# A two-layer hybrid transformer on one core: the last feed-forward sublayer by plain products instead of seven block products

## The chip, the core and the metric

The kernel runs on one core of a Trainium2 chip, as a single program. The core has a matrix engine (PE, with its weight loads shown apart as PEld), a vector engine (DVE), a scalar engine (ACT), a general engine (POOL), an engine that here issues the transfers (SP), and 16 DMA engines. The metric is the device time of one execution in microseconds. Three runs of the kernel before gave 3025.62, 3025.64 and 3031.76 us.

## The reference

Two streams, 512 tokens of `x` and 256 tokens of `ctx`, each 1024 wide, pass through two layers. A layer has three sublayers: a feed-forward one, a mixer (attention, state space and retention side by side), and a second feed-forward one. Only `x` is returned, so the last layer's second feed-forward sublayer works on 512 tokens alone.

```python
def swiglu(h, wg, wu, wd):
    return (jax.nn.silu(h @ wg) * (h @ wu)) @ wd

def sublayer_in(h, m, i):
    return h * (1.0 + m[..., i, 1, :]) + m[..., i, 0, :]

def residual(h, sub, m, i, g, b):
    return layer_norm(DEEPNORM_ALPHA * h + (1.0 + m[..., i, 2, :]) * sub, g, b)
...
        x = residual(x, 0.5 * swiglu(sublayer_in(x, m_l, 2), ffn_w_gate[l, 1], ffn_w_up[l, 1], ffn_w_down[l, 1]),
                     m_l, 2, norm_g[l, 2], norm_b[l, 2])
```

The gate and up weights are 1024 x 2816, the down weights 2816 x 1024, all in fp32.

## The kernel before

**Order of the work.** The six sublayers follow each other; sublayer (l, i) is layer l, place i, so the last one is (1, 2). The program is written as a sequence, but a planner orders each engine's instructions anew when it is built, by a simulated timeline (`schedule_with_timeline_sim=True`, L1669): what comes first in the text has priority, and what would have to wait in that simulation is passed by what is ready. On the chip each engine then runs its list strictly in that order. All transfers that matter here are on the queue of SP.

**Precision.** Every fp32 operand is split into two fp16 pieces, a first one (ACT, L320 for weights, L445 for activations) and the remainder (DVE, L321 and L446), and each product takes the three passes (first, first), (first, second), (second, first), `PASSES`. One block of pieces has 512 weight columns (or 2 x 256, or 4 x 128) on 128 partitions, with both pieces.

**Feed-forward sublayer (`ffn`, L357).** The 2816 hidden columns are 11 pairs of 128, and the pairs are in five groups, `GROUPS = [[0, 1], [2, 3], [4, 5], [6, 7], [8, 9, 10]]`. For each pair there are the gate and the up product, silu and their product; after each group the down products of its pairs are added to `acc`; after the last group comes the norm.

- *Seven products.* For pairs 1 to 10 the gate and up products go by Winograd's form of Strassen's scheme: the weights in four blocks (column tile, half of the features), the input in four blocks (half of the features, half of the tokens), and seven block products instead of eight. `load` (L408) makes the sums S1 to S4 of weight blocks on POOL (L414 to L417) and splits seven blocks into pieces. `gate_up` (L476) runs seven products of 12 matmuls each for gate and for up (L494) and combines them on DVE (L499, one copy on ACT, L510). The differences of the input's blocks are made once per sublayer by `input_differences` (L466, DVE and POOL L454 to L460) from an fp32 copy of the input that the norm before stored in DRAM (L301, `keep`) and that is loaded again (L472).
- *Down products of groups 0 to 3* go the same way: `prep_down` (L382) makes sums of weight blocks on POOL (L391 to L394) and seven blocks of pieces, `put_act` (L429) makes sums of activation blocks on POOL (L437 to L440) and seven blocks of pieces, and `down_blocks` (L705) runs seven products for each token tile of a half (L719) and combines them on DVE and POOL (L726, L731, L733, L734).
- *Plain form.* Pair 0 of every sublayer but the first goes by plain products (`gate_up_plain`, L541, matmuls L555): for each of two column tiles, gate and up with 8 feature tiles x 3 passes, into a PSUM buffer ("big", two of them) that holds both; `silu_up` (L424) then reads it. It leaves PE busy while the input differences are made. In the last sublayer it does the first three token tiles ahead of the fourth, which arrives late. The last group's down products are plain too (`down_last`, L768, matmuls L781).

**Buffers.** Raw weights come by transfers of 1 MB into two buffers ("raw"). Blocks of pieces have 16 buffers "pc", which all sublayers share, and 5 buffers "pcd" in the pool of the sublayer itself; `ring` (L372) deals them out in turn, in proportion. The sublayer's own pool can only be used once the sublayer before is done with its own. `load_plain` (L404) uses `prep` (L341), which takes "pc" buffers only.

**How far ahead.** `prepare` (L803) works off a list of jobs, one transfer of weights and its pieces each, in the order of use, and keeps `FIT` = 3 jobs ahead of the pair or group that uses them.

Of the kernel before, what the change touches and what calls it, by code (L numbers as in the profile page):

```python
# [43 lines left out]
def kernel(  # L44
# [25 lines left out]
    class Tags:  # L70
        """Allocators of one phase: a rotating set of buffers for each kind of use."""
# [36 lines left out]
    def condition(alloc):  # L108
        """Loads the vectors that the whole network needs as columns, and takes them to columns."""
# [39 lines left out]
        # ALPHA times the gains and biases of the norms, as rows in DRAM  # L149
# [5 lines left out]
    def ada_vec(l, v, alloc):  # L155
        """One conditioning vector of both streams."""
# [32 lines left out]
    def gate_bcast(l, i, n, alloc):  # L189
        """The scaled gate rows of sublayer (l, i) on all partitions, for each of n streams."""  # L190
        res = []
        for r in range(n):
            gt = alloc([P, D], f"gate{l}{i}{r}")
            nc.sync.dma_start(out=gt, in_=gate_rows[l, i][r].partition_broadcast(P))
            res.append(gt)
        return res

# [1 line left out]
    def affine_cols(l, i, prev):  # L199
        """Columns (scale, bias) that take the normalised rows to SA * (input of sublayer (l, i))."""  # L200
# [11 lines left out]
    def to_pieces(dst, src32):  # L212
        """src32 [P, KC, P] fp32 -> dst [P, 2, KC, P] fp16 pieces."""
        V.tensor_copy(dst[:, 0], src32)
        V.tensor_tensor(out=dst[:, 1], in0=src32, in1=dst[:, 0], op=ALU.subtract)

    def turn(yh, t, cols, nm, alloc):
        """Rows of tile t -> transposed fp32 input of a sublayer, in two halves of its features."""
# [22 lines left out]
    class Stream:  # L241
        """The residual stream between sublayers: ALPHA times its rows in DRAM (the first one's without ALPHA), and
        the sublayer's transposed input where that is wanted again."""
# [6 lines left out]
    class Norm:  # L250
        """The normalisation that ends sublayer (l, i), and what follows from it, tile by tile in two stages."""

        def __init__(self, l, i, nxt, last, arow, ayh, au32):
# [5 lines left out]
            if not last:  # L259
# [3 lines left out]
                self.keep = nxt[1] != 1  # L263

        def one(self, t, rt):
            """rt: the residual sum of tile t."""
# [45 lines left out]
    def block(shape, nm, dt=F16):  # L312
        """Room for the fp16 pieces of 512 weight columns (in several row tiles) or so."""
        return main.tile([P, 2] + shape, dt, tag="pc", name=f"pc{nm}", bufs=NBLOCK)
# [8 lines left out]
    class Pieces:  # L323
        """Pieces of a weight block, two row tiles in each buffer."""
# [7 lines left out]
    def load_raw(src, a, b, nm):  # L332
        """src may be a list of blocks that lie side by side."""
# [16 lines left out]
    # Gate and up products go by Winograd's form of Strassen's 2 x 2 x 2 scheme: with W^T in blocks A11, A12, A21, A22  # L350
    # (column tile, half of the features) and the input in B11, B12, B21, B22 (half of the features, half of the
    # tokens), seven block products of fp16 pieces give the four blocks of W^T u.
    # The down products of all but the last group of pairs go the same way: activations in blocks (half of the tokens,
    # column tile), weights in blocks (column tile, half of the output features).
    GROUPS = [[0, 1], [2, 3], [4, 5], [6, 7], [8, 9, 10]]

    def ffn(l, i, uT, stream, ntiles, nxt, last, todo):  # L357
# [5 lines left out]
        with tc.tile_pool(name=f"ffn{l}{i}", bufs=1) as fp:  # L363
# [8 lines left out]
            def ring(shape, nm):  # L372
                """A block of pieces from the two sets of buffers in turn, in proportion to their numbers."""
# [6 lines left out]
            plain = GROUPS[-1]  # L380
# [23 lines left out]
            def load_plain(pr_):  # L404
                wt[pr_] = [prep(columns(src, pr_), KC, 256, f"gu{l}{w}_{pr_}{q}")
                           for q, src in enumerate((ffn_w_gate, ffn_w_up))]

            def load(pr_, q):  # L408
                nm = f"gu{l}{i}_{pr_}{q}"
                raw = load_raw(columns((ffn_w_gate, ffn_w_up)[q], pr_), KC, 256, nm)  # L410
# [18 lines left out]
            def put_act(pr_, sg, spare):  # L429
                """Pieces of the activations sg of a pair, in blocks as its down products want them."""  # L430
# [17 lines left out]
            # differences of the input's blocks, as pieces  # L448
            tt = {}

            def differences(b11, b12, b21, b22, k, cols, shape, nm):
                """Blocks k, columns cols of the differences, from the fp32 input."""
# [23 lines left out]
            def gate_up(pr_):  # L476
# [5 lines left out]
                for q, dst in enumerate((sg, up)):  # L482
# [22 lines left out]
                    # the first pair leaves time for the differences, the last one starts with the first tokens  # L505
# [35 lines left out]
            def gate_up_plain(pr_):  # L541
# [17 lines left out]
                # the last token tile of a short stream comes late: it waits for the others' products  # L559
                if not has_ctx:  # L560
# [3 lines left out]
                for cc in range(2):  # L564
                    for pp, lo, hi in parts[cc]:
                        if not has_ctx:
# [6 lines left out]
            def first_pair():  # L573
                """The conditioning of the first sublayer, its input and its first pair of column blocks, which
                proceed together through the blocks of two feature tiles as these arrive."""
# [129 lines left out]
            def down_blocks(gi, prs):  # L705
                """Adds the down products of a group of pairs to acc."""
# [39 lines left out]

            def gate_rows_of(h):
# [7 lines left out]
            def residual(h):  # L755
                """Half h of acc: ALPHA times the stream plus the gated products so far."""
# [40 lines left out]
            # the weights go through the buffers in the order of their use  # L797
# [13 lines left out]
            else:  # L811
                load_plain(0)
                input_differences()
            prepare(FIT)
            for gi, prs in enumerate(GROUPS):
                for q in prs:
                    if todo and (q > 1 or len(todo) >= NPAIR - 1 - q):
                        ada_vec(*todo.pop(0), al("ada"))
                    if q > 0:
                        gate_up(q)  # L820
                    else:
                        if start:
                            finish()
                        else:
                            gate_up_plain(0)
# [5 lines left out]
                if gi < len(GROUPS) - 1:  # L831
                    down_blocks(gi, prs)
# [6 lines left out]
    class Fill:  # L839
        """Projection work that is laid between the steps of the chains, as generators that yield their cost."""  # L840
# [28 lines left out]
    class Skew:  # L869
        """Generators that advance together, each one step behind the one that came after it."""  # L870
# [20 lines left out]
    def mixer(l, uT, stream, nxt, last):  # L891
# [5 lines left out]
        with tc.tile_pool(name=f"mix{l}", bufs=1) as mp:  # L897
# [10 lines left out]
            # weights of the projections, in the order of their use  # L908
# [18 lines left out]
            def mm_T(pp, pc, cc, lo, hi):  # L927
                """Transposed projection of one 128-column chunk."""
# [8 lines left out]
            def mm_tok(pp, pc, t, n_=256):  # L937
                """Projection of 256 columns for one token tile."""
# [18 lines left out]
            # per-layer scalars on all partitions  # L957
# [39 lines left out]
            def rv_tile(t):  # L997
                """Values of the retention branch and raw steps of the state-space branch, one token tile."""
# [120 lines left out]
            def put_state(Hs, t, pst):  # L1119
                """The state of chunk t goes to the slot of the chunk that it enters."""  # L1120
# [94 lines left out]
            class Rope:  # L1215
                """A transposed projection whose first S columns are rotated."""
# [169 lines left out]
            def attend(h, t):  # L1386
# [21 lines left out]
                # both maps share the first one's row sum, which the output takes up  # L1408
# [265 lines left out]
```

## Time and profile before

| what | value |
|---|---|
| median of the runs | 3025.64 us |
| the profiled execution: span from its first to its last instruction | 3023.2 us |
| mean granted clock of PE | 0.966 |
| last feed-forward sublayer: first matmul of pair 0 | 2567.6 us |
| end of its pair 0, about | 2592.8 us |
| its last matmul ends | 3014.2 us |
| its matmuls, pairs 1 to 10 and down products | 2160 |

The page of a profile gives the busy time of each engine; a stretch of the span can be asked for alone. In a group of instructions the columns are line, engine, operation, output and inputs, shapes and count, then busy us and mean ns of one, then the idle time of the engine just before them and what ended it. In the order of time a row has start, length, engine, line, operation and count, and in brackets the idle time before it with the instruction that ended it. A matmul's own duration includes its way through the array, so rates are read from runs of many.

### The profile page before, as it was taken

To read this page: it belongs to the slowest core of one execution; us is meant where nothing else is said; L and a number is where in the kernel's file an instruction comes from. 1 tells how busy PE (TensorE), PEld (TensorE's weight loads), DVE (VectorE), ACT (ScalarE), POOL (GpSimd) and SP (SyncE) were. 2 spreads that over 40 slices of the span, in tenths; PEclk is the share of its full clock that TensorE was granted. 3 is DMA by queue.
4 is the path that set the end of the run, shared out by engine and by line. 5 is a ranking of instruction groups with operands and counts; after the bars stand their busy time and mean duration, and the time that the engine had idled before them with its cause. 6 is when DMAs were issued, how large, how long until landed. Compare 5 with 4: busy or idle time off the path is not lost. (4 is left out here: it accounts for less than half of the span.)

```text
span 3023.2 us, 45096 instructions
## 1 busy us (share of the span) xinstructions
PE 2666.6 (88%) x17087; PEld 1615.5 (53%) x17087; DVE 2538.8 (84%) x3677; ACT 1224.7 (41%) x2602; POOL 1544.6 (51%) x1296
## 2 busy tenths in 40 slices
PE   6799999989899979999999889888999998777778
PEld 4444444557677834444444444444556677555455
DVE  4988888886867788898789988898887777899998
ACT  3443343434447343343233443343335374444332
POOL 1646557132525464566725646567232444656672
PEclk9899999999999999999999999999999999899999
DMA  7253354333233253453372322122333342322222
GB/s 230 70 176 124 112 189 147 104 116 92 72 96 99 100 180 117 134 195 120 111 244 104 133 70 68 45 84 94 105 113 112 91 112 92 133 83 84 70 79 89
DMA packets 221519, 346.97 MB, mean 115 GB/s; under 512 B 16136, under 2 KB 162294, under 8 KB 221302
## 3 DMA queue, kind: packets, MB, share of 16 engines
q1 hardware_dynamic: 221302, 344.09, 35.3%
q8 instruction: 134, 2.20, 0.3%
q14 instruction: 83, 0.68, 0.1%
HBM read 303.52 MB, written 25.31 MB: 109 GB/s over the span
## 5 line engine op out<-in xcount | busy, mean ns | idle before, releaser
L494 PEld LDWEIGHTS <-pcgu 128*128 128x128 f16 x5088 | 500.4, 100 | 440.4 <-issue 181.2
L494 PE MATMUL m<-T,pcgu 128*128 128x384 f16 (+1 forms) x2400 | 410.7, 318 | 43.5 <-DVE U L499 31.1
L719 PE MATMUL pd<-pcd,act 128*128 128x512 f16 x1452 | 367.0, 392 | 76.9 <-DVE act L446 23.1
L719 PEld LDWEIGHTS <-act 128*128 128x128 f16 x1848 | 183.3, 100 | 343.2 <-issue 112.1
L494 PE MATMUL x<-uT,pcgu 128*128 128x384 f16 (+1 forms) x1512 | 254.8, 318 | 39.3 <-DVE sg L499 16.7
L321 DVE SCALAR_TENSOR_TENSOR pcgu<-rawgu,pcgu 128x512 f16<-128x512 f32 x208 | 237.6, 1156 | 16.6 <-ACT pcgu L320 16.4
L734 POOL TENSOR_TENSOR acc<-acc,D 128x512 f32<-128x512 f32 x132 | 188.9, 1443 | 71.0 <-DVE acc L733 70.6
L494 PEld LDWEIGHTS <-pegu 128*128 128x128 f16 x1632 | 160.4, 100 | 118.2 <-issue 36.0
L417 POOL TENSOR_TENSOR S4gu<-rawgu,S2gu 128x512 f32<-128x512 f32 x80 | 113.4, 1417 | 181.5 <-DVE pcgu L321 178.3
L414 POOL TENSOR_TENSOR S1gu<-rawgu 128x512 f32<-128x512 f32 x80 | 115.9, 1449 | 109.0 <-DMA rawgu<-in_ffn_w_gate_dram 55.5
L415 POOL TENSOR_TENSOR S2gu<-S1gu,rawgu 128x512 f32<-128x512 f32 x80 | 119.8, 1497 | 89.2 <-DVE pcgu L321 72.8
L416 POOL TENSOR_TENSOR S3gu<-rawgu 128x512 f32<-128x512 f32 x80 | 123.2, 1540 | 77.9 <-DVE pegu L321 54.5
L320 ACT ACTIVATE pcgu<-rawgu 128x512 f16<-128x512 f32 x208 | 125.6, 623 | 65.3 <-PE m L494 18.6
L942 PEld LDWEIGHTS <-uT 128*128 128x128 f16 x1344 | 133.7, 100 | 32.8 <-issue 12.6
L781 PE MATMUL pd<-pcd,act 128*128 128x512 f16 x594 | 144.7, 379 | 4.2 <-DVE dt L787 3.8
L94 POOL TENSOR_SCALAR rs<-mv 128x1 f32<-128x1 f32 x32 | 16.3, 508 | 240.5 <-DVE mv L273 240.5
L228 ACT ACTIVATE u<-pt,abc 128x128 f32<-128x128 f32 x224 | 81.5, 467 | 141.3 <-PE pt L225 95.5
L321 DVE SCALAR_TENSOR_TENSOR pcd<-rawd,pcd 128x512 f16<-128x512 f32 x132 | 135.4, 1039 | 0.8 <-ACT pcd L320 0.5
L446 DVE TENSOR_TENSOR act<-sg,act 128x384 f16<-128x384 f32 (+1 forms) x141 | 131.4, 963 | 2.2 <-ACT act L445 2.2
L781 PEld LDWEIGHTS <-act 128*128 128x128 f16 x792 | 77.4, 98 | 99.4 <-issue 12.6
L494 PE MATMUL x<-T,pcgu 128*128 128x384 f16 (+1 forms) x672 | 119.6, 320 | 11.8 <-DVE sg L499 6.5
L726 DVE TENSOR_TENSOR D<-D,pd 128x512 f32<-128x512 f32 x132 | 89.9, 681 | 46.6 <-PE pd L719 45.1
(375 smaller groups left out, 6403.5 us busy)
## 6 DMA issues: line engine op xcount, KB each, us to landing
adaw<-in_ada_w_dram SPq DMA_DIRECT2D x128, 512.0 KB
rawd<-in_ffn_w_down_dram SPq DMA_DIRECT2D x44, 1024.0 KB
rawgu<-in_ffn_w_gate_dram SPq DMA_DIRECT2D x43, 1024.0 KB
rawgu<-in_ffn_w_up_dram SPq DMA_DIRECT2D x43, 1024.0 KB
row<-yh SPq DMA_DIRECT2D x56, 256.0 KB
rawwo<-in_w_out_dram SPq DMA_DIRECT2D x8, 1024.0 KB
inp<-u SPq DMA_DIRECT2D x16, 512.0 KB
u<-inp SPq DMA_DIRECT2D x16, 512.0 KB
```

The lines of the kernel that those rows point to most:

```text
L320: A.activation(pc[:, 0], src, AF.Copy, scale=SW)
L321: V.scalar_tensor_tensor(out=pc[:, 1], in0=src, scalar=SW, in1=pc[:, 0], op0=ALU.mult, op1=ALU.subtract)
L414: G.tensor_tensor(out=s1, in0=a21, in1=a22, op=ALU.add)
L415: G.tensor_tensor(out=s2, in0=s1, in1=a11, op=ALU.subtract)
L416: G.tensor_tensor(out=s3, in0=a11, in1=a21, op=ALU.subtract)
L417: G.tensor_tensor(out=s4, in0=a12, in1=s2, op=ALU.subtract)
L446: V.tensor_tensor(out=pc[:, 1], in0=src, in1=pc[:, 0], op=ALU.subtract)
L494: PE.matmul(pp, lhsT=blocks[m][:, a, k, :], rhs=rhs, start=(n == 0), stop=(n == 11))
L719: PE.matmul(pd, lhsT=acts[q][m][:, a, ts], rhs=wd[q][m][:, b], start=(n == 0), stop=(n == len(prs) * 3 - 1))
L734: G.tensor_tensor(out=c_, in0=c_, in1=part, op=ALU.add)
L781: PE.matmul(pd, lhsT=acts[q][2 * cc + hf][:, a, o:o + P], rhs=wd[q][2 * cc + h][:, b], start=(n == 0), stop=(n == len(prs) * 6 - 1))
L942: PE.matmul(pp, lhsT=uT[:, a, k, t * P:(t + 1) * P], rhs=pc.at(b, k, 0, n_), start=(n == 0), stop=(n == KC * 3 - 1))
```

## The change

In the last feed-forward sublayer, (1, 2), all pairs and groups use the plain form. `gu_plain` and `plain` name the pairs whose weights and activations are split without sums: all of them there; in the other sublayers pair 0 (gate and up) and the last group (down), as before. `load` and `load_plain` now share one path, in which the blocks of plain weights come from `ring`, so also from "pcd" buffers; that holds for pair 0 in the sublayers (0, 2) and (1, 0) too. The mixer before the last sublayer no longer stores the fp32 input for the differences, and these are not made there. Only pair 0 still treats the late token tile apart. A new function, `down_plain`, adds the plain down products of groups 0 to 3: a matmul group of 12 per token tile and half of the output, copied to `acc` by ACT in group 0 and added by DVE afterwards.

```diff
-                self.keep = nxt[1] != 1
+                self.keep = nxt[1] != 1 and nxt != (DEPTH - 1, 2)
...
-            plain = GROUPS[-1]
+            whole_plain = not has_ctx
+            gu_plain = set(range(NPAIR)) if whole_plain else {0}
+            plain = set(range(NPAIR)) if whole_plain else set(GROUPS[-1])
...
             def load_plain(pr_):
-                wt[pr_] = [prep(columns(src, pr_), KC, 256, f"gu{l}{w}_{pr_}{q}")
-                           for q, src in enumerate((ffn_w_gate, ffn_w_up))]
+                for q in range(2):
+                    load(pr_, q)
 
             def load(pr_, q):
                 nm = f"gu{l}{i}_{pr_}{q}"
-                raw = load_raw(columns((ffn_w_gate, ffn_w_up)[q], pr_), KC, 256, nm)
+                src = columns((ffn_w_gate, ffn_w_up)[q], pr_)
+                if pr_ in gu_plain:
+                    raw = load_raw(src, KC, 256, nm)
+                    blocks = []
+                    for j in range(0, KC, 2):
+                        blocks.append(ring([2, 256], f"{nm}{j}"))
+                        split_weight(blocks[-1], raw[:, j:j + 2, :])
+                    wt.setdefault(pr_, []).append(Pieces(blocks))
+                    return
+                raw = load_raw(src, KC, 256, nm)
...
-                if not has_ctx:
+                late = not has_ctx and pr_ == 0
+                if late:
...
+            def down_plain(gi, prs):
+                for t in range(ntiles):
+                    hf, o = t // (ntiles // 2), (t % (ntiles // 2)) * P
+                    for h in range(2):
+                        pd = sm([P, 512], f"pd{l}{i}_{gi}{t}{h}")
+                        n = 0
+                        for q in prs:
+                            for cc in range(2):
+                                for a, b in PASSES:
+                                    PE.matmul(pd, lhsT=acts[q][2 * cc + hf][:, a, o:o + P],
+                                              rhs=wd[q][2 * cc + h][:, b],
+                                              start=(n == 0), stop=(n == len(prs) * 6 - 1))
+                                    n += 1
+                        c_ = acc[t][:, h * 512:(h + 1) * 512]
+                        if gi == 0:
+                            A.copy(c_, pd)
+                        else:
+                            V.tensor_tensor(out=c_, in0=c_, in1=pd, op=ALU.add)
...
                 load_plain(0)
-                input_differences()
+                if not whole_plain:
+                    input_differences()
...
-                    if q > 0:
-                        gate_up(q)
+                    if start and q == 0:
+                        finish()
                     else:
-                        if start:
-                            finish()
-                        else:
-                            gate_up_plain(0)
+                        (gate_up_plain if q in gu_plain else gate_up)(q)
+                    if q == 0:
                         new_acc()
...
-                    down_blocks(gi, prs)
+                    (down_plain if whole_plain else down_blocks)(gi, prs)
```

The other lines of the diff take out comments and docstrings.

More of the change, by code (lines that the diff above doesn't have):

```diff
@@ L565, in gate_up_plain @@
                     for pp, lo, hi in parts[cc]:
-                        if not has_ctx:
+                        if late:
                             mm(pp, cc, S - P, S, S - P)
```

## The prediction

> **What bounds the kernel now.** First the page's totals, then the busy time of each engine in stretches, for all engines are loaded in a mean over stages that differ.
>
> ```profile
> span 3023.2 us, 45096 instructions
> ...
> PE 2666.6 (88%) x17087; PEld 1615.5 (53%) x17087; DVE 2538.8 (84%) x3677; ACT 1224.7 (41%) x2602; POOL 1544.6 (51%) x1296
> ```
>
> Stretches (columns: stretch, length, PE, weight loads, DVE, ACT, POOL busy with counts, granted clock, DMA share, GB/s):
>
> ```profile
> 2593.00:3014.20 421.20, 325.95 (x2160) 218.77 (x2159) 393.60 (x539) 162.77 (x322) 248.50 (x179) 0.92 0.27 87
> ...
> 2593.00:2620.00 27.00, 9.81 (x62) 6.46 (x62) 26.04 (x25) 14.69 (x30) 20.61 (x14) 0.81 0.45 158
> ...
> 2991.00:3014.00 23.00, 23.00 (x108) 10.29 (x106) 21.75 (x34) 0.41 (x1) 5.62 (x6) 1.00 0.18 69
> 1656.00:1686.00 30.00, 28.53 (x185) 18.20 (x184) 25.58 (x28) 11.84 (x27) 20.45 (x15) 1.00 0.63 228
> ...
> 1095.00:1615.00 520.00, 470.77 (x2892) 234.03 (x2891) 446.83 (x601) 190.60 (x344) 279.19 (x204) 0.98 0.45 151
> ```
>
> The first row is the sublayer that is changed, from the end of its pair 0 to its last matmul. DVE is busy 393.6 of 421.2 us (93%), PE 77% at a clock of 0.92. So VectorE sets the pace. What PE waits for there says the same:
>
> ```profile
> PE m L494 <- DVE U L499: 19.0, 11, 3.4
> PE pd L719 <- DVE act L446: 18.2, 15, 2.6
> ...
> PE pd L719 <- DVE pcd L321: 6.0, 1, 6.0
> ```
>
> The long waits are for combinations of products and for activation pieces. For weight pieces PE waited 6.0 us, once. Why DVE is so slow shows in its costliest instruction, the second piece of a weight block (L321), in this sublayer and in the mixer (min/median/max ns):
>
> ```profile
> L321 DVE SCALAR_TENSOR_TENSOR pcgu<-rawgu,pcgu x42: 677/1217/1762, 2598.5 to 2966.9; 128x512 f16<-128x512 f32 x42
> ...
> L321 DVE SCALAR_TENSOR_TENSOR pcwo<-rawwo,pcwo x16: 678/683/1344, 2412.0 to 2482.6; 128x512 f16<-128x512 f32 x16
> ```
>
> The same work takes 0.68 us undisturbed and a median of 1.22 us here, where POOL is busy 248.5 us with sums of blocks.
>
> **PE: the term that I expect to decide.** The 2160 matmuls of the first row are 1680 of 256 columns (10 pairs x 2 x 7 products x 12), 336 of 512 (4 groups x 2 x 7 x 12) and 144 of 512 in the last group. Back-to-back rates come from runs in the order of time:
>
> ```profile
> 2981.41 2.56 PE L494 MATMUL m<-T,pcgu 128*128 128x256 f16 x22
> ...
> 2983.81 1.47 PE L494 MATMUL x<-T,pegu 128*128 128x256 f16 x12
> ...
> 2989.46 0.59 PE L781 MATMUL pd<-pcd,act 128*128 128x512 f16 x2
> ...
> 2997.85 4.70 PE L781 MATMUL pd<-pcd,act 128*128 128x512 f16 x21
> ```
>
> 256 columns: (2.56 - 1.47) / 10 = 0.109 us. 512 columns: (4.70 - 0.59) / 19 = 0.216 us. Before: 1680 x 0.109 + 480 x 0.216 = 286.8 us, of 421.2. After, a pair is 2 x 2 x 24 = 96 matmuls of 512 columns, a group 4 x 2 x 12 = 96, the last group is as it was: 960 + 384 + 144 = 1488 x 0.216 = **321.4 us**. The change adds 34.6 us of matmul time and still lies 99.8 us below the present 421.2.
>
> **DVE, ACT and POOL after.** Weight pieces: 80 blocks for pairs 1 to 10 and 44 for the down products, 124 where there were 208. At 0.683 us: 84.7 us. The other terms:
>
> ```profile
> L733 DVE TENSOR_TENSOR acc<-acc,pd 128x512 f32<-128x512 f32 x24 | 16.3, 678 | 4.2 <-PE pd L719 4.2
> ...
> L766 DVE TENSOR_TENSOR acc<-acc,xt 128x512 f32<-128x512 f32 x8 | 7.3, 916 | 0.4 <-DMA xt<-row 0.4
> ...
> L426 DVE SCALAR_TENSOR_TENSOR sg<-pl,sg x2: 676/680/683, 2594.6 to 2607.3; 128x512 f32<-128x512 f32 x2
> ...
> L446 DVE TENSOR_TENSOR act<-sg,act x8: 415/416/425, 2976.3 to 2992.7; 128x256 f16<-128x256 f32 x8
> ```
>
> 24 adds of down products 16.3, 22 products of gate and up at 0.68 = 15.0, 44 activation pieces at 0.416 = 18.3, the residual 7.3, the last group and norm some 22 (DVE's 21.75 in 2991 to 3014): 164 us, half of PE's 321. Gone are all L499, L726, L454 to L460. POOL keeps the residual's 8 products and the norm's columns, so what DVE waits for on its shared path goes too. If the 124 pieces still took 1.22 us, DVE would be at 231 us, still under PE. ACT, busy 162.8 us now, loses as many first pieces as DVE loses second ones. The next to be late is therefore PE itself.
>
> **Waits that the plain form has.** gate_up_plain holds both large PSUM buffers for a pair; the next pair's first column tile waits for silu and product of this pair's first, which have 48 x 0.216 = 10.4 us while the second runs. A group's down products use two buffers, 12 matmuls (2.6 us) each, freed by one add of 0.68 us behind at most a few pieces on DVE. Both loops are in the trace: 1656 to 1686 is gate_up_plain (28.53 of 30 us busy) and 2991 to 3014 the last group's plain products (23.00 of 23). Weights: 8 blocks of pieces per 20.7 us stage, 21 buffers, so one stage in use and one ahead. One megabyte:
>
> ```profile
> 2555.27 5.66 DMA rawgu<-in_ffn_w_gate_dram
> ...
> L320 ACT ACTIVATE pcd<-rawd 128x512 f16<-128x512 f32 x33 | 18.9, 614 | 5.5 <-DMA rawd<-in_ffn_w_down_dram 5.5
> ```
>
> A transfer of 5.66 us and 4 blocks of pieces (4 x 0.614 and DVE's last 0.683) are 8.8 us a job even one after the other; 31 jobs are 273 us, below 321. I divide PE's sum by a **dense share of 0.96**. Bounds: 0.99 (2991 to 3014) and 0.90, the sublayer of 1095 to 1615 (470.77 of 520) with DVE heavily loaded. 321.4 / 0.96 = 334.8 us.
>
> **Pair 0 in three sublayers.** load_plain now goes through ring, whose fifth block (index 4, the first of up's four) is a "pcd" buffer of the sublayer's own pool. That pool opens only when the sublayer before has written its last row:
>
> ```profile
> 1086.04 0.63 ACT L320 ACTIVATE pegu<-S1gu 128x512 f16<-128x512 f32 x1 [5.93 <-DMA row<-yh]
> ...
> 1674.53 0.63 ACT L320 ACTIVATE pegu<-S1gu 128x512 f16<-128x512 f32 x1 [8.25 <-DMA row<-yh]
> ...
> 2589.19 0.63 ACT L320 ACTIVATE pegu<-S1gu 128x512 f16<-128x512 f32 x1 [6.16 <-DMA row<-yh]
> ```
>
> So up's products of pair 0 start 1.3 us (both pieces) after that and take half of the pair. In the last sublayer that half is 48 x 0.216 = 10.4 us. There POOL loses the block sums that lay between the norm's steps:
>
> ```profile
> 2573.65 1.26 POOL L417 TENSOR_TENSOR S4gu<-rawgu,S2gu 128x512 f32<-128x512 f32 x1 [0.63 <-DVE pcgu L321]
> 2574.88 0.57 POOL L95 TENSOR_TENSOR rs<-rs,nhalf 128x1 f32<-128x1 f32 x1
> 2575.41 1.28 POOL L414 TENSOR_TENSOR S1gu<-rawgu 128x512 f32<-128x512 f32 x1
> 2577.98 1.59 POOL L415 TENSOR_TENSOR S2gu<-S1gu,rawgu 128x512 f32<-128x512 f32 x1 [1.30 <-DVE pcgu L321]
> ...
> 2584.80 7.96 PE L555 MATMUL pl<-uT,pcgu 128*128 128x384 f16 x111
> ```
>
> I take the pool 4.5 us earlier (0 to 7; 1.26 + 1.28 + 1.59 of sums and DVE's shorter waits): 2584.7 + 1.3 + 10.4 = 2596.4, against 2592.8 now: 3.6 us late. The four stores and loads of kept inputs go too, off PE's path.
>
> In the two earlier sublayers pair 0 ends now with
>
> ```profile
> 1090.11 5.40 PE L555 MATMUL pc<-uT,pcgu 128*128 128x256 f16 x48
> ...
> 1681.14 5.40 PE L555 MATMUL pc<-uT,pcgu 128*128 128x256 f16 x48
> ```
>
> There half of pair 0 is 48 x (0.216 + 0.109) = 15.6 us: it ends at 1086.0 + 1.3 + 15.6 = 1102.9 instead of 1095.5 (+7.4), and at 1691.4 instead of 1686.5 (+4.9). Two raw buffers are also held longer, up's by block 4 and the next pair's gate weights by block 8, so two transfers of 1 MB move behind the pool's opening, on queue SP ahead of or among the loads of kept inputs; at the rate of that stretch they are 7 us more:
>
> ```profile
> 1086.00:1095.00 9.00, 9.00 (x75) 7.12 (x73) 5.27 (x7) 5.35 (x9) 3.76 (x3) 1.00 0.81 290
> ...
> 1107.89 0.48 PE L494 MATMUL x<-T,pegu 128*128 128x384 f16 x1 [4.69 <-ACT T L459]
> ...
> 1114.11 0.80 PE L494 MATMUL m<-T,pcgu 128*128 128x384 f16 x2 [5.74 <-ACT T L459]
> ```
>
> PE waits 10.4 us for the differences there anyway, which hides the late end unless the differences come late as well. So 0 to 14.6 us each, and 3 below nothing since the planner orders everything anew; I take 5 each, near the lower rows, **10 us** in all.
>
> **The sum.**
>
> ```profile
> 3013.39 0.81 PE L781 MATMUL pd<-pcd,act 128*128 128x512 f16 x3
> ```
>
> The last matmul ends at 3014.2, the span at 3023.2: 9.0 us of tail, unchanged.
>
> 2596.4 + 334.8 + 9.0 + 10 = 2950.2 us of span. The median of the runs, 3025.64, lies 2.4 above the profiled span: **2952.6 us**, 2.4% faster. Bounds of the terms: at best 2592.8 + 324.6 + 9.0 + 2.4 = 2929, at worst 2599.4 + 357.1 + 9.0 + 2.4 + 20 = 2988.
>
> **Rivals.**
> (1) *The clock does not recover.* It is 0.92 in this stage and 0.81 where PE idles (2593 to 2620). If PSUM hand-overs keep PE pausing, 334.8 / 0.92 = 363.9 and the time is 2982. Against it: 1.00 in 2991 to 3014, where the same two buffers change hands every 3.9 us. The Trainium skill, "TensorE: Matmul & The Clock Gate", section "A second HAM failure mode: psum-queue depth-cycling", says that 512-column matmuls cycling through PSUM banks can pause often enough for the clock gate to fall back between bursts; that last row does not show it. Chance 0.10.
> (2) *Nothing is lost in the earlier sublayers and PE is dense at 0.99*: 2929 to 2935. Chance 0.12.
> (3) *Weights come just in time, no longer ahead* (slower). If 21 buffers don't cover a stage ahead, because blocks come free only as its last products end, each of 14 stages (10 pairs, 4 groups) waits for a transfer and eight pieces, 5.66 + 8 x 0.614 + 0.683 = 11.3 us: 158 us in place of the 13.4 of the dense share, 3097 us. It is slower than before from 6.2 us a stage ((73.0 + 13.4) / 14). For it: the raw buffers are two, and blocks of a pair are freed only in its second column tile. Against it: 6.0 us of such waits in the whole stage now, with DVE at 93%. Chance 0.04; pieces alone exposed (5.6 us a stage, 3018), about no change, 0.03.
> (4) *The change doesn't do what it says*: DVE stays the bound since pieces and hand-overs serialise in its queue, at its present 1.22 us. 231 us of work cannot fill 421, so it could only spoil PE's dense share, to some 0.90: 357.1 in place of 334.8, 2975. Chance 0.03.
>
> **How the numbers follow.** Forecast (2940 to 2975) 0.68, rivals 0.10, 0.12, 0.04 + 0.03, 0.03. Range 2927 to 2988. A measurement of this kernel tells about 0.2% (6 us) from no change: faster 0.93, within 0.03, slower 0.04.
>
> **What would show it.** Right: in the last sublayer PE over 93% busy at a clock near 1.00 over about 335 us, DVE near half, POOL nearly idle, L321 at 0.68; up's products of pair 0 begin about 1.5 us after the last row's transfer in three sublayers. Wrong: PE waits on L320 or L321 more than 1 us per stage (rival 3); clock under 0.95 with PE busy (rival 1); the first matmul of the last mixer shifted by more than 30 us or to earlier times (pair 0's term).

## The result

The changed kernel takes 2932.15 us (median of four runs, 2929.58 to 2939.95) where the kernel before, on the same chip, takes 3027.14: a ratio of 0.9694, with a 95% interval of 0.9677 to 0.9711. It is 3.1% faster. The forecast was 2952.6, in a range of 2927 to 2988.

The profiled execution of the changed kernel is the slowest of the four: 2939.95 us, with a span of 2938.1. The page's lines for it, engines first and then the chain that ended last:

```profile
span 2938.1 us, 43039 instructions
...
PE 2667.3 (91%) x16415; PEld 1546.5 (53%) x16415; DVE 2290.2 (78%) x3383; ACT 1154.3 (39%) x2466; POOL 1296.5 (44%) x1124
...
PE 11%; DMA 1%; DVE 0%; POOL 0%; ACT 0%; issue 0%; DVEq 0%; POOLq 0%; SPq 0%; ACTq 0%
```

PE is busy as long as it was (2667.3 us against 2666.6), in a span that is 85 us shorter; DVE lost 249 us and POOL 248. The chain followed back from the last instruction led mostly over DVE before:

```profile
DVE 9%; PE 3%; issue 1%; POOL 1%; DMA 1%; ACT 0%; DVEq 0%; POOLq 0%; SPq 0%; ACTq 0%
```

Now it is mostly PE (11% of the span): from 2606 us to the last matmul it holds matmuls alone. Stretches of the changed kernel's last sublayer say why (columns as before: PE, weight loads, DVE, ACT, POOL, clock, DMA share, GB/s):

```profile
2571.50:2588.20 16.70, 11.15 (x56) 6.15 (x55) 7.99 (x11) 3.58 (x10) 6.73 (x6) 0.81 0.09 32
2588.20:2595.00 6.80, 6.79 (x26) 3.42 (x27) 1.28 (x2) 0.47 (x1) 0.00 (x0) 0.61 0.86 257
2595.00:2604.10 9.10, 9.10 (x120) 7.55 (x118) 4.66 (x8) 4.99 (x9) 0.00 (x0) 1.00 1.05 396
2604.00:2929.20 325.20, 323.15 (x1491) 145.90 (x1488) 148.56 (x245) 97.90 (x187) 16.46 (x14) 0.99 0.30 99
```

The last row answers to the 421.2 us that the prediction began with. From the end of pair 0 to the last matmul it is 325 us now, PE is busy 99% of it at a clock of 0.99, DVE 46%, POOL 5%. In that stretch PE waited once, and the second weight pieces are short again (min/median/max ns):

```profile
PE pl L567 <- DVE sg L438: 2.0, 1, 2.0
```

```profile
L321 DVE SCALAR_TENSOR_TENSOR pcgu<-rawgu,pcgu x55: 679/692/1758, 2613.9 to 2855.7; 128x512 f16<-128x512 f32 x55
L321 DVE SCALAR_TENSOR_TENSOR pcd<-rawd,pcd x31: 683/686/693, 2603.8 to 2876.8; 128x512 f16<-128x512 f32 x31
```

So the bound has moved from VectorE to PE. What took VectorE so long, and whether the plain form was needed to free it, the experiments had to tell.

### The profile page after: what moved, and what is told of

Its sections match the earlier page's. It is cut to its first block, busy times and chain, and to the rows that moved or that the text cites. A ratio compares the mean times of both kernels' runs of the same rounds, so it can differ in the third digit from the quotient of the medians.

```text
span 2938.1 us, 43039 instructions
## 1 busy us (share of the span) xinstructions
PE 2667.3 (91%) x16415; PEld 1546.5 (53%) x16415; DVE 2290.2 (78%) x3383; ACT 1154.3 (39%) x2466; POOL 1296.5 (44%) x1124
## 5 line engine op out<-in xcount | busy, mean ns | idle before, releaser
L506 PE MATMUL m<-T,pcgu 128*128 128x384 f16 x1920 | 354.2, 329 | 21.7 <-DVE U L511 9.9
L732 PE MATMUL pd<-pcd,act 128*128 128x512 f16 x1188 | 296.0, 385 | 51.1 <-DVE acc L746 20.5
L732 PEld LDWEIGHTS <-act 128*128 128x128 f16 x1512 | 149.1, 99 | 261.7 <-issue 96.1
L567 PE MATMUL pl<-uT,pcgu 128*128 128x512 f16 (+2 forms) x1068 | 228.8, 368 | 10.2 <-DVE uT L214 8.1
L747 POOL TENSOR_TENSOR acc<-acc,D 128x512 f32<-128x512 f32 x108 | 151.1, 1413 | 64.2 <-DVE acc L746 64.2
L798 POOL TENSOR_TENSOR acc<-acc,gate 128x512 f32<-128x512 f32 x44 | 62.7, 1430 | 256.0 <-DVE acc L778 255.8
L506 PEld LDWEIGHTS <-pegu 128*128 128x128 f16 x1248 | 119.6, 98 | 106.4 <-issue 31.0
L506 PE MATMUL x<-uT,pcgu 128*128 128x384 f16 x864 | 159.5, 332 | 12.3 <-DVE sg L511 5.2
L974 PEld LDWEIGHTS <-uT 128*128 128x128 f16 x1344 | 135.1, 101 | 33.2 <-issue 12.1
L814 PE MATMUL pd<-pcd,act 128*128 128x512 f16 x594 | 141.1, 379 | 3.1 <-DVE dt L820 3.1
L814 PEld LDWEIGHTS <-act 128*128 128x128 f16 x792 | 77.5, 98 | 99.3 <-issue 11.3
L427 POOL TENSOR_TENSOR S2gu<-S1gu,rawgu 128x512 f32<-128x512 f32 x60 | 90.9, 1516 | 82.2 <-DVE pcgu L321 63.8
L426 POOL TENSOR_TENSOR S1gu<-rawgu 128x512 f32<-128x512 f32 x60 | 85.1, 1419 | 80.2 <-DMA rawgu<-in_ffn_w_gate_dram 59.8
```

The lines of the kernel that those rows point to most:

```text
L426: G.tensor_tensor(out=s1, in0=a21, in1=a22, op=ALU.add)
L427: G.tensor_tensor(out=s2, in0=s1, in1=a11, op=ALU.subtract)
L506: PE.matmul(pp, lhsT=blocks[m][:, a, k, :], rhs=rhs, start=(n == 0), stop=(n == 11))
L567: PE.matmul(pp[:, j, o:o + hi - lo], lhsT=wp.at(a, k, cc * P, (cc + 1) * P), rhs=uT[:, b, k, lo:hi], start=(n == 0), stop=(n == KC * 3 - 1))
L732: PE.matmul(pd, lhsT=acts[q][m][:, a, ts], rhs=wd[q][m][:, b], start=(n == 0), stop=(n == len(prs) * 3 - 1))
L747: G.tensor_tensor(out=c_, in0=c_, in1=part, op=ALU.add)
```

## The experiments

Ratios are to the kernel before on the same chip (medians of 3023 to 3027 us); an interval is 95%. Diffs are against the changed kernel where nothing else is said.

### Half of the change alone

Only gate and up plain, down products by the seven products:

```diff
-            plain = set(range(NPAIR)) if whole_plain else set(GROUPS[-1])
+            plain = set(GROUPS[-1])
...
-                    (down_plain if whole_plain else down_blocks)(gi, prs)
+                    down_blocks(gi, prs)
```

> In the last sublayer gate and up are plain, the down products of groups 0 to 3 stay with seven products. PE's own work is then 960 x 0.216 + 480 x 0.216 = 311 us, DVE's some 265 us (148 weight blocks, 68 activation blocks, 56 combinations), part of it held up by POOL's remaining sums. Theory (DVE's load and POOL's disturbance bounded the sublayer, and most of both sat in gate and up): most of the gain remains, about 2940 us (2925 to 2960). Rival (the turns from gate and up to down and back cost the time): most of the gain is gone, 2985 or more.

Measured: 2933.69 us, ratio 0.970 [0.9683, 0.9716]: the whole gain, within the uncertainty. The stretch of gu_only, and the waits of PE in it:

```profile
2600.00:2925.00 325.00, 314.30 (x1440) 141.10 (x1439) 241.89 (x326) 117.03 (x234) 125.54 (x99) 0.99 0.30 99
```

```profile
PE pl L567 <- DVE sg L438: 5.7, 2, 5.0
PE pd L732 <- DVE acc L744: 2.8, 1, 2.8
PE pd L732 <- DVE acc L746: 2.5, 1, 2.5
```

The seven products save 48 matmuls of 512 columns here (an eighth of 384), 10.4 us, and PE is indeed busy 9 us less than in the changed kernel; the waits give it back.

Only the down products plain:

```diff
-                self.keep = nxt[1] != 1 and nxt != (DEPTH - 1, 2)
+                self.keep = nxt[1] != 1
...
-            gu_plain = set(range(NPAIR)) if whole_plain else {0}
+            gu_plain = {0}
...
-                if not whole_plain:
-                    input_differences()
+                input_differences()
```

> In the last sublayer only the down products are plain, gate and up of pairs 1 to 10 stay with seven products. PE's own work is 297 us, DVE's about 375 us with POOL's sums beside it. Theory: DVE stays the bound, 375 / 0.95 = 395 us in place of 421, so about 2998 us (2985 to 3012). Rival (the turns between gate and up and down cost the time): 2965 or less.

Measured: 2946.4 us, ratio 0.9743 [0.9726, 0.976]. The theory's size was wrong. The time lies in the rival's range, but the rival's reason, the turns between gate and up and down, does not hold: gu_only has such turns too and keeps the whole gain. With the seven products of the down part went 32 sums of weight blocks, 32 of activations and 24 adds into `acc` on POOL, by the groups of the kernel before 50 + 33 + 36 = 119 us of its 248.5 in that stretch, and the combinations on DVE; that was enough to bring DVE below PE. The stretch of down_only:

```profile
2596.00:2936.00 340.00, 307.75 (x2207) 217.45 (x2206) 288.78 (x454) 139.04 (x270) 130.25 (x90) 0.98 0.30 100
```

DVE is busy 288.8 of 340 us (85%), 105 us less than before, and PE 307.75 (91%), while DVE's pieces of gate and up weights are still slow beside the sums that remain (median 1.21 us). Each half by itself brings most of the gain, and the two don't add: either takes DVE's busy time below PE's. In down_only PE still stands 32 us of its stretch, 28 of them in waits for DVE.

### What POOL's sums cost

The kernel before, with the sums of blocks left out in the last sublayer, so that the same products take unsummed blocks. The diff is against the kernel before, with one of the sums shown for all:

```diff
+            def pool_sum(out_, x_, y_, op):
+                if not has_ctx:
+                    return x_
+                G.tensor_tensor(out=out_, in0=x_, in1=y_, op=op)
+                return out_
...
-                G.tensor_tensor(out=s1, in0=a21, in1=a22, op=ALU.add)
+                s1 = pool_sum(s1, a21, a22, ALU.add)
...
-                            G.tensor_tensor(out=c_, in0=c_, in1=part, op=ALU.add)
+                            if has_ctx:
+                                G.tensor_tensor(out=c_, in0=c_, in1=part, op=ALU.add)
```

> The kernel before, with all sums on POOL of weight blocks, activation blocks and down products left out in the last sublayer (raw blocks are taken in their place, so its products are other ones); matmuls, pieces and combinations on DVE are as many as before. Theory (POOL's sums hold up DVE's instructions with two operands in SBUF): DVE's instructions fall to their undisturbed 0.68 and 0.42 us, its work to about 315 us against PE's 287, and the sublayer to about 325 us; the time is about 2930 us (2915 to 2955), as good as the changed kernel. Rival (the number of DVE's instructions and their chains decide): above 2985 us.

Measured: 2919.79 us, ratio 0.9653 [0.9632, 0.9673]. The seven products without POOL's sums beat the plain form by 0.4%. That can have two reasons: DVE runs freely, or nobody waits for a sum any more. The next run is like this one, with the sums made and thrown away and the adds into `acc` as they were. The diff is against no_sums, without the lines of those adds:

```diff
             def pool_sum(out_, x_, y_, op):
-                if not has_ctx:
-                    return x_
                 G.tensor_tensor(out=out_, in0=x_, in1=y_, op=op)
-                return out_
+                return out_ if has_ctx else x_
```

> The kernel before, with the sums of weight and activation blocks in the last sublayer still made by POOL, as many and as large as before, but used by nobody: the products take unsummed blocks in their place (so the output is another). Only the adds into acc on POOL stay in use. It tells apart the two ways in which leaving the sums out can have brought 103 us. Theory (POOL's instructions beside DVE's stretch those that read two operands from SBUF): the stretching stays, the median of the second weight pieces at 1.1 us or more, and the time is within some 35 us of before, 2990 or more. Rival (DVE and ACT stood waiting for the sums, a chain from transfer to POOL to pieces): pieces as slow as before but nobody waits, 2920 to 2955.

Measured: 3040.15 us, ratio 1.0043 [1.0028, 1.0058]. All the gain is gone although nobody uses a sum of blocks. The same stretch of the two, no_sums first:

```profile
2598.00:2911.00 313.00, 295.45 (x2160) 212.08 (x2159) 277.39 (x535) 160.30 (x320) 19.31 (x16) 0.99 0.34 113
```

```profile
2599.00:3030.00 431.00, 331.77 (x2160) 223.29 (x2159) 390.17 (x539) 161.88 (x321) 250.04 (x178) 0.90 0.26 87
```

The same 2160 matmuls and practically the same DVE instructions (535 and 539): with POOL busy 250 us beside it, DVE takes 390 us for what it does in 277. The stretch is 118 us longer and DVE's busy time 113; DVE is idle for nearly as long in both (36 and 41 us). The groups of DVE instructions show which of them. From no_sums (mean ns behind the comma):

```profile
L321 DVE SCALAR_TENSOR_TENSOR pcgu<-rawgu,pcgu 128x512 f16<-128x512 f32 x98 | 67.9, 711 | 7.9 <-ACT pcgu L320 7.2
...
L452 DVE TENSOR_TENSOR act<-sg,act 128x256 f16<-128x256 f32 x68 | 24.7, 415 | 0.5 <-ACT act L451 0.5
...
L739 DVE TENSOR_TENSOR acc<-acc,pd 128x512 f32<-128x512 f32 x24 | 16.3, 680 | 2.6 <-PE pd L725 2.5
```

and from thrown_sums:

```profile
L321 DVE SCALAR_TENSOR_TENSOR pcgu<-rawgu,pcgu 128x512 f16<-128x512 f32 x98 | 108.7, 1133 | 7.6 <-ACT pcgu L320 7.6
L450 DVE TENSOR_TENSOR act<-sg,act 128x256 f16<-128x256 f32 x68 | 49.8, 784 | 0.5 <-ACT act L449 0.5
...
L737 DVE TENSOR_TENSOR acc<-acc,pd 128x512 f32<-128x512 f32 x24 | 16.3, 679 | 2.6 <-PE pd L723 2.5
```

The instructions whose two operands are both in SBUF (weight pieces, activation pieces) grow from 711 to 1133 and from 415 to 784 ns. The add that takes one operand from PSUM (`pd`) stays at 680. So it isn't the wait for a sum that cost the kernel its time, but what POOL's work takes from VectorE. The 24 adds into `acc` on POOL (33.5 us), which thrown_sums has and no_sums has not, are part of that work; their share was not measured apart.

The other way round, the changed kernel with idle sums of weight blocks put onto POOL. `idle_sums`, not shown here, makes four sums of the four blocks of a weight tile, and nobody uses them:

```diff
+                    if whole_plain and pr_ not in GROUPS[-1]:
+                        idle_sums([b11, b12, b21, b22], [P, 512], f"d{nm}")
...
+                    if whole_plain and pr_ > 0:
+                        idle_sums([raw[:, kh * 4:kh * 4 + 4, cc * P:(cc + 1) * P]
+                                   for cc in range(2) for kh in range(2)], [P, 4, P], nm)
```

> The changed kernel, with POOL also making the four sums of each weight block in the last sublayer (pairs 1 to 10, groups 0 to 3) that the seven products would need, and nobody using them. Theory (in the plain form PE is the bound at 99% and DVE, at 46%, has room for stretched pieces): the median of the second weight pieces rises above 1 us, DVE to some 200 us, and the time stays within 10 us of the changed kernel, up to 2942. Rival (the gain is freedom from POOL itself, whatever PE does): 25 us or more above the changed kernel, 2957 or more.

Measured: 2955.54 us, ratio 0.976 [0.9745, 0.9774], above the changed kernel by 20 us by the ratios, 23 by the medians: twice what the theory allowed, a little less than the rival asked. Stretch and waits of idle_sums:

```profile
2604.00:2945.00 341.00, 323.89 (x1494) 145.39 (x1492) 228.17 (x248) 95.70 (x187) 172.21 (x118) 0.99 0.28 94
```

```profile
PE pl L579 <- DVE sg L450: 6.9, 1, 6.9
PE pd L782 <- DVE act L470: 5.3, 3, 1.8
PE pd L782 <- ACT act L469: 4.9, 4, 3.2
```

The second pieces of gate and up weights are long again (median 1.24 us). DVE is busy 80 us longer and still at 67%. Its throughput doesn't bind; but silu's product and the activation pieces, which PE needs next, come later, and PE waits 17 us where it waited 2. The plain form stands the sums far better than the seven products (20 us for 156 us more of POOL, against 120 us for 231 between no_sums and thrown_sums), yet room on an engine does not make its delays free.

### Pair 0

Pair 0's weights in the shared "pc" buffers again, in all three sublayers:

```diff
-                for q in range(2):
-                    load(pr_, q)
+                wt[pr_] = [prep(columns(src, pr_), KC, 256, f"gu{l}{w}_{pr_}{q}")
+                           for q, src in enumerate((ffn_w_gate, ffn_w_up))]
```

> As the changed kernel, but the weights of pair 0 go into buffers that all sublayers share, as they did before the change, in all three sublayers. Theory: the profile of the changed kernel shows pair 0 of the last sublayer ending 11 us later than before (3.9 us of shift from earlier and 7.4 us of its own), because one block waits for the pool; without that wait the time falls by 6 to 11 us, to about 2923 us (2920 to 2927). Rival (that wait is covered, the shift is the planner's): within 3 us of the changed kernel's 2932.

Measured: 2933.98 us, ratio 0.9701 [0.9683, 0.9718], no difference to the changed kernel. The delay that I had priced went, and the wait behind it grew from 2.01 to 4.84 us. In the order of time, PE's rows of the changed kernel:

```profile
2588.21 2.74 PE L567 MATMUL pl<-uT,pegu 128*128 128x384 f16 x8 [5.16 <-ACT pegu L320]
2590.74 4.47 PE L567 MATMUL pl<-uT,pcgu 128*128 128x384 f16 x18
2595.05 0.81 PE L567 MATMUL pl<-uT,pegu 128*128 128x384 f16 x4
2595.70 4.43 PE L567 MATMUL pl<-uT,pcgu 128*128 128x384 f16 x42
...
2600.30 2.51 PE L567 MATMUL pl<-uT,pcgu 128*128 128x128 f16 x42
2602.64 0.50 PE L567 MATMUL pl<-uT,pegu 128*128 128x128 f16 x6
...
2606.15 1.74 PE L567 MATMUL pl<-uT,pegu 128*128 128x512 f16 x6 [2.01 <-DVE sg L438]
```

and PE's rows of pair0_pc:

```profile
2577.74 16.25 PE L567 MATMUL pl<-uT,pcgu 128*128 128x384 f16 x162
2598.83 7.03 PE L567 MATMUL pl<-uT,pcgu 128*128 128x512 f16 x24 [4.84 <-DVE sg L438]
```

and ACT's:

```profile
2595.51 0.63 ACT L320 ACTIVATE ped<-rawd 128x512 f16<-128x512 f32 x1 [9.04 <-DMA rawd<-in_ffn_w_down_dram]
2596.16 1.28 ACT L437 ACT_TABLE_LOAD   x1
2597.45 0.60 ACT L437 ACTIVATE sg<-pl 128x512 f32<-128x512 f32 x1
```

Without the wait PE finishes pair 0 at 2594.0 and then stands 4.84 us, because both PSUM buffers are full. ACT's silu is behind first pieces of a down weight that came by a transfer (9.04 us of waiting for it), and behind a table load of 1.28 us. From the first product of the sublayer to the first of pair 1 it is 30.9 us (2567.95 to 2598.83) instead of 34.7 (2571.50 to 2606.15). These 4 us don't appear in the medians. Why is not shown: one execution of each kernel was profiled, and the start of the sublayer differs by more than that between them. It is at 2571.50 in the changed kernel and at 2564.44 in gu_only, whose source up to there is the same.

### The same change in more or less of the kernel

Gate and up of six pairs by seven products again:

```diff
-            gu_plain = set(range(NPAIR)) if whole_plain else {0}
+            gu_plain = {0, 1, 2, 3, 10} if whole_plain else {0}
...
-                if not whole_plain:
-                    input_differences()
+                input_differences()
```

> The changed kernel, with gate and up of pairs 4 to 9 of the last sublayer by seven products again; pairs 0 to 3 and 10 and all down products stay plain. POOL then makes 48 sums of weight blocks where there were 112 and those of activations. Six pairs save 12 matmuls of 512 columns each way of 96: 6 x (96 x 0.216 - 168 x 0.109) = 14.5 us of matmul time. Theory (DVE has room between, so PE stays the bound): 8 to 15 us less than the changed kernel, 2917 to 2927. Rival (seven products bring back stretched pieces and waits for combinations that eat the gain): within 5 us of the changed kernel or above it.

Measured: 2935.73 us, ratio 0.9696 [0.9682, 0.9711]: nothing gained, as the rival had it. PE is busy 11 us less in its stretch and idle for 16 of 328 us, where it was idle for 2:

```profile
2597.00:2925.00 328.00, 312.12 (x1927) 188.16 (x1925) 234.26 (x372) 124.45 (x240) 87.51 (x62) 0.99 0.32 103
```

The plain form in sublayer (1, 0) too (768 tokens):

```diff
-                self.keep = nxt[1] != 1 and nxt != (DEPTH - 1, 2)
+                self.keep = nxt[1] != 1 and nxt[0] != DEPTH - 1
...
-            whole_plain = not has_ctx
+            whole_plain = l == DEPTH - 1
```

> The changed kernel, with the plain form also in the first feed-forward sublayer of the second layer, (1, 0), of 768 tokens. There the sublayer takes 518 us from the end of its pair 0 to its last matmul, with seven products that are 428 us of matmul at the back-to-back rates; plain they are 488, and 495 at the dense share of 0.985. Theory (with POOL's sums gone PE alone sets the pace): 518 - 495 = 23 us less, 2905 to 2920. Rival (that sublayer is held by the work of other parts that the planner lays into it, which stays): within 6 us of the changed kernel, or slower by the added 60 us of matmul.

Measured: 2905.78 us, ratio 0.9593 [0.9577, 0.9609]: a further 1.0%, at the lower end of the theory's range. The term worked out before the run held: from the end of pair 0 to its last matmul the sublayer takes 489.9 us (1687.5 to 2177.4), where 495 were expected and the changed kernel takes 517.8 (1691.2 to 2209.0).

And in (0, 2) as well (`whole_plain = (l, i) != (0, 0)`, `keep` never):

> Like plain_10, and the plain form also in the second feed-forward sublayer of the first layer, (0, 2). There PE makes six of the second layer's conditioning vectors as well, which stay. In the changed kernel PE is busy 467.9 of the 511 us from the end of its pair 0 (1104 to 1615), so only 43 us are to be had, while the plain form adds 60 us of matmul. Theory (PE is the bound where POOL's sums are gone, at a dense share near 0.99): (467.9 + 60) / 0.99 - 511 = 22 us more than plain_10, 2915 to 2935. Rival (what POOL's sums cost there is more than the trace's idle PE time shows): equal to plain_10 or faster.

Measured: 2900.36 us, ratio 0.9588 [0.9574, 0.9603], equal to plain_10: the rival. PE is now busy nearly throughout that sublayer; the stretch in plain_02:

```profile
1104.00:1630.00 526.00, 522.68 (x3263) 271.25 (x3262) 191.95 (x325) 122.63 (x233) 40.06 (x36) 1.00 0.42 136
```

From the end of pair 0 to its last matmul the sublayer takes 538.8 us (1096.0 to 1634.8), where plain_10, with seven products there, takes 542.3 (1101.4 to 1643.7): the 22 us expected are not there. My sum had counted PE's 467.9 busy us as matmul time at full clock. At the 0.98 of that sublayer (in the prediction's row of 1095 to 1615) 2% of them, 9 us, were the clock, which is 1.00 now. The rest isn't explained by a run.

Last, gate and up plain but the down products of groups 0 to 3 by seven products (the edit of gu_only), first in both sublayers of the second layer:

> Like plain_10, with the down products of groups 0 to 3 by seven products again in both sublayers of the second layer. They save an eighth of 576 + 384 matmuls of 512 columns: 26 us of matmul time, and bring back POOL's sums of down weights and activations. Theory (in the last sublayer gate and up alone came out as the whole change, so the saved matmuls were paid back in waits and stretched pieces): within 8 us of plain_10, 2898 to 2914. Rival (in (1, 0) with half again as many tokens per weight DVE has room for it): 10 to 20 us less than plain_10.

Measured: 2891.78 us, ratio 0.9559 [0.9543, 0.9574]. Here the rival was right: 14 us less than plain_10 by the medians, 10 by the ratios, of the 15.6 us of matmul that the down products save in (1, 0). In the traces that sublayer, from the end of pair 0 to its last matmul, is 15.5 us shorter (474.4 against 489.9), with DVE busy 306.9 us of it (65%). That it is the number of tokens per weight that leaves this room was not tested apart. This is the fastest version that leaves nothing out, 4.4% under the kernel before, and it beats the changed kernel by 1.4%. With (0, 2) in the same form:

> Gate and up plain, down products of groups 0 to 3 by seven products, in all three later feed-forward sublayers: (0, 2) joins gu_10. Theory (in plain_02 PE is busy 522.7 of 526 us there, so the down products' 576 / 8 x 0.216 = 15.6 us of matmul time saved come off the time, as they did in (1, 0), and the plain gate and up cost what plain_02 cost against plain_10, within 6 us): 2870 to 2890. Rival (the conditioning vectors, whose instructions are also on DVE and POOL, leave no room for the sums): 2890 to 2910.

Measured: 2913.15 us, ratio 0.9628 [0.9612, 0.9644], slower than gu_10 by 0.7% and above both ranges. The longest waits of PE in (0, 2) of gu_02 are for the weights of the conditioning vectors:

```profile
PE ada L162 <- DMA adaw<-in_ada_w_dram: 26.2, 11, 7.0
PE pd L732 <- DVE acc L746: 4.8, 1, 4.8
```

The same wait is 0.3 us in plain_02, and 12.0 in gu_10, which has seven products there for gate and up too. So what is missing doesn't look like room for the sums, as the rival had it (DVE is busy 279.6 of 526 us): transfers became late. Why they come latest in this order was not tried and stays open.

## Why the prediction was right, and where its sizes were off

**The bound.** The step that decided was that PE takes over at 321.4 us of matmul and DVE falls far below. It held: 325.0 us from the end of pair 0 (2604.1) to the last matmul (2929.1), DVE at 148.6 us against 164 estimated. The reason named for DVE's slowness, POOL's sums, was argued there; no_sums and thrown_sums show it.

**The dense share** was the term that was mis-sized most: 321.4 / 325.0 is 0.989, not 0.96, 9.8 us less than the 334.8 predicted. The row nearest in kind stood in the prediction, the last group's plain products at 23.00 of 23 us. I moved away from it towards a sublayer where DVE was loaded with seven products, which by my own reckoning no longer applied.

**Pair 0.** In the changed kernel it ends 11.3 us later than before: 3.9 of it come from ahead of the sublayer (2571.50 against 2567.6), and 7.4 are its own, where 3.6 had been predicted. The opening of the pool was right: the first piece in a "pcd" buffer is made at 2587.52, which is 2583.6 without the shift, against 2584.7 predicted. What failed is the size of what is still to come then, half of pair 0 at 48 x 0.216 = 10.4 us. The fourth token tile is late, so all of its 96 matmuls of 128 columns are still to come, beside 48 of 384: at 0.163 us (4 from 2595.05 to 2595.70) and 0.056 us (42 from 2600.30 to 2602.64) that is 7.8 + 5.4 = 13.2 us. And after the wait the first 26 take 6.8 us instead of 26 x 0.163 = 4.2, at a granted clock of 0.61. Together these are 15.8 of the 15.9 us from 2588.2 to the end of pair 0. By the medians the term is worth nothing, as pair0_pc showed.

**The two earlier sublayers**, priced at 10 us, cost less than the executions differ: the last sublayer begins 3.9 us later than before in the profile of the changed kernel and 3.2 earlier in that of gu_only. Their pair 0 did end about where the prediction put it, at 1104.1 and 1691.2 us (1102.9 and 1691.4 predicted); what it costs the later sublayers was put too high. The wait for the input's differences hid part of the late end of pair 0, which had been the reason for the lower bound: in (0, 2) PE waits 7.0 us for them in the changed kernel, 10.4 before.

**The sum** by the rows: 2592.8 + 3.9 + 7.4 + 325.0 + 9.0 = 2938.1. The tail of 9.0 us held. The predicted 2950.2 is 12.1 above it: 9.8 too much for the dense share and 6.1 for the earlier sublayers, 3.8 too little for pair 0. So the errors cancelled in part, by luck. A further 8.3 us come from the step to the median, which was put 2.4 us above the profiled span and lies 5.9 below it, since the slowest of the four runs was the profiled one. The upper end of the range was added up too low for its own terms: a pool that opens no earlier gives 2589.2 + 1.3 + 10.4 = 2600.9, not 2599.4, and 14.6 for each of the two earlier sublayers gives 29, not 20.

**The rivals.** (2), dense at 0.99 and nothing lost earlier, was nearest: 2929 to 2935 holds the median. (1), a clock that does not recover, fell: 0.99 over the whole stretch, with PSUM buffers changing hands every 2.6 to 10.4 us. The rule on PSUM-queue cycling in the Trainium skill, "TensorE: Matmul & The Clock Gate", section "A second HAM failure mode: psum-queue depth-cycling", which stood beside it, is not borne out at this spacing. (3), weights just in time, fell: no wait of PE for weight pieces in the stretch. (4) fell with DVE's 46%.

One thing the prediction never asked: whether the plain form was what brought the gain. Its 34.6 us of added matmuls are a price, paid for the sums that go. no_sums, with less matmul work (286.8 us against 321.4 at the prediction's rates) and no sums, is faster still; but it is no version to keep, since it leaves out what the seven products need.

## What to carry to other kernels

An engine that shows busy for 93% may be standing for part of it: compare an instruction's median with its minimum, and look which engine works beside it, before counting the work as work. A scheme that saves matmuls and pays in element-wise sums can only pay while VectorE, slowed by what POOL does beside it, stays below PE; taking back half of it was enough here, and which form was best differed from sublayer to sublayer. When a wait at a hand-over is taken away, look for what else opens at the same moment: here 5.16 us were taken away, and the next wait grew from 2.01 to 4.84.

## What the runs showed of the hardware

POOL's element-wise instructions slowed only those of VectorE that read both operands from SBUF: means of 711 to 1133 and 415 to 784 ns between no_sums and thrown_sums, while adds with one operand in PSUM stayed at 680 and 679. A single second piece took 677 ns at least and 1764 at most, an added 1.09 us. The Trainium skill, "SBUF — State Buffer", section "SBUF: two separate sides", says that such a VectorE instruction and a GpSimd instruction exclude each other for the whole of one of them; the means and the untouched PSUM adds agree. What I had not expected is the price in all: 231 us more of POOL's instructions cost VectorE 113 us.

After the wait of 5.16 us in pair 0 the granted clock was 0.61 over the next 6.8 us and then 1.00, which made 26 matmuls 2.6 us longer. Shorter waits cost PE time afterwards too. Behind the 4.84 us in pair0_pc, and behind the 2.01 us ahead of pair 1 in the changed kernel, the next 24 matmuls of 512 columns took 6.9 us in place of 24 x 0.216 = 5.2, at a mean clock of 0.75 (pair0_pc first):

```profile
2598.83:2605.69 6.86, 6.86 (x24) 2.74 (x24) 4.98 (x10) 3.62 (x9) 0.00 (x0) 0.75 0.90 319
```

```profile
2606.15:2613.02 6.87, 6.87 (x25) 2.74 (x25) 4.06 (x9) 4.09 (x9) 0.00 (x0) 0.75 0.73 256
```

So a wait of 2 to 5 us cost PE another 1.7 to 2.6 us after it was over. The Trainium skill, "TensorE: Matmul & The Clock Gate", section "What's actually happening", puts the fall of the clock at an idle window of some 3.4 us; the waits of 5.16 and 4.84 us agree with it, and the fall behind the wait of 2.01 us does not follow from that figure alone.
